# Inverse roots by ScalarE's square root and one Newton step in three places, by integer start and three Newton steps in the others; the opening's modulation dealt out by single weight blocks, with another order of transfers

## The chip, the cores and the metric

The kernel runs on one core of a Trainium2 chip. The metric is the device time of one execution in microseconds, of the slowest core; with one core it is that core's time. Five engines share the work and run their own queues in program order: TensorE (PE, matrix products, with PEld as its weight load), VectorE (DVE), ScalarE (ACT), GpSimd (POOL) and SyncE (SP), which here only issues transfers.

## The reference

One layer of a diffusion backbone over 512 latent tokens of width 1024 with a context of 256 tokens. It computes, cut to what matters here:

```
mod_x = split(silu(c) @ w_mod + b_mod, 6)          # six vectors of 1024; mod_c likewise from c_ctx
rms_norm(x, w) = x * rsqrt(mean(x*x) + 1e-6) * w
h   = rms_norm(x, mix_pre_norm) * (1 + mod_x[1]) + mod_x[0]
cq, ckv, kr, z, xbc, dt = split(h @ w_in)          # 384, 256, 32, 1024, 1536, 32
attn = latent attention (queries from rms_norm(cq), keys and values from rms_norm(ckv), context keys too)
ssd  = rms_norm(y * silu(z)),  y = two-way state-space scan over xbc, dt
x   = x + mod_x[2] * rms_norm([attn, ssd] @ w_out, mix_post_norm)
h   = rms_norm(x, ffn_pre_norm) * (1 + mod_x[4]) + mod_x[3]
gate, val = split(h @ w_up)                        # 2816 each
x   = x + mod_x[5] * rms_norm((gelu(conv3(gate)) * val) @ w_down, ffn_post_norm)
```

The context goes through the same first modulation and input projection (with mod_c), and gives keys, values and the scan's start states. Everything is fp32.

## The kernel before

**Products.** Each fp32 product is made of three faster ones. An operand is split into a high and a low part (`split`, L493 to L498: ACT copies the value to the rounded type, L497; DVE subtracts, L498), and TensorE adds high by high, high by low and low by high in one accumulator. The modulation and the token sums use plain fp32 products.

**Order.** The code is a recording: all instructions are first listed, then a planner (`price`, `dependences`, `Graph`, with lists of hints named `pins`, `urgent` and `holds`) prices each one, simulates the engines, chooses an order for every engine's queue, the transfers among them, and a place in memory for every block, and the program is built in that order. So an edit in one place lets the planner arrange all of it anew. `pins` fix one group of instructions behind another, `urgent` groups go first, and `holds` keep a group back. Loads are issued by SP (`load`, L489) except where `nc.scalar` is given, which is ACT's queue.

**Opening.** PE starts with dummy products on zeros (L677; `IDLE` gives their numbers in three places). Meanwhile the transfers bring c and c_ctx (as `cv`, and once more as `c2`), the transposed tokens `xt` in eight blocks of 128 columns by 512 tokens, the constants `cst` and the parameters `prm` (norm weights and b_mod). The steps:

- `spread` (L656) makes silu(c) a row over all partitions by eight products; the row stays in PSUM as `pv` and is copied to `cs`.
- `token_scale`: squares of the eight blocks on ACT (L608), their additions on DVE (L610), sums over the partitions by products with ones (L616), the mean (DVE, L620), the inverse root (`rsqrt`), eight products that lay the result out as rows over all partitions (`rows_of`, L534), and a copy of those rows, `rB`, by ACT (L627).
- The modulation is needed as a column per block k of 128 features: shift and scale. `modcolumn` loads a weight block (512 KB); `moddot` (L586) is a DVE product with the row of silu(c), summed along the row; `moddots` (L596) does it on PE instead, eight products of 128x64 per weight, for c and c_ctx at once. `ON_PE = 2, 4, 6` sends both weights of these blocks to PE; the other blocks' dots for c_ctx are done later, from the weights kept.
- `modulated` finishes a block: L632 adds b_mod, L633 multiplies (1 + scale) by the norm's weight, L638 scales the tokens by the column and by the row of inverse roots, L639 adds the shift and rounds to the high part (ACT), L642 makes the low part (DVE).
- `half_of_z` (L685): twelve products of the block with the first half of the z columns of w_in. The blocks come in the order `BLOCKS = 0, 2, 1, 4, 3, 6, 5, 7`. `silu_of_z` (L691, L692) and the second half of z follow.

**The inverse root.** All of them go through `rsqrt`, on a column (or four to six columns) of 128 values:

```
G.tensor_tensor(out=yt, in0=x, in1=powers[:, :n], op=ALU.pow)                      # L521, powers = -0.5
V.tensor_scalar(out=x, in0=x, scalar1=-0.5, scalar2=None, op0=ALU.mult)            # L522
V.scalar_tensor_tensor(out=tt, in0=yt, scalar=yt, in1=x, op0=ALU.mult, op1=ALU.mult)  # L524
V.scalar_tensor_tensor(out=yt, in0=tt, scalar=1.5, in1=yt, op0=ALU.add, op1=ALU.mult) # L528
```

that is, a power on POOL and one Newton step on DVE. It is used for the tokens and the context tokens (`token_scale`), for the two latents (cq and ckv), at the end of the scan (`ssd_finish`), twice for each of four token tiles around the output projection (`sumsq`), and once for each tile at the very end (`last`).

**Middle.** Input projections (`gemm_T`, L758), the scan, attention (L1181 to L1236), then the output projection (`natural_gemm`, L1295). The remaining modulation vectors are made by DVE dots beside it (`modblock`). `modfinish` turns the gate vector (with the norm's weight, L1275 to L1278) into a row: the column is written to DRAM in `mod_rows` (L1282) and read back to all partitions (L1284), both on ACT's queue:

```
nc.scalar.dma_start(out=scratch[n].rearrange("j p -> p j"), in_=ms)                # L1282
nc.scalar.dma_start(out=row, in_=scratch[n:n+1]... .to_broadcast([P, D]))          # L1284
```

**The turn into the MLP.** For each of four token tiles `after_mix` takes the sums of squares of the projection (ACT, L1347; L1349 or L1351), an inverse root, the product with the gate row (L1360; for the last tile's second half L1362 on ACT and L1363 on POOL), the residual (L1375), squares and an inverse root again, and the scaling by the row of 1 + scale (L1379). `transposes` (L1387) turns the tile, and L1390 and L1391 add the shift and make the high and low parts. Then come the up projection (`gemm_T`, L758, with `gated` behind it), and the down projection (L1482) with the last norm: squares L1502, the product with the gate row L1503, L1466, the inverse root, the residual L1472 and the store.

Of the kernel before, what the change touches and what calls it, by code (L numbers as in the profile page):

```python
# [18 lines left out]
P = 128  # L19
D = 1024  # L20
# [68 lines left out]
ON_PE = 2, 4, 6  # L89
BLOCKS = 0, 2, 1, 4, 3, 6, 5, 7  # L90
IDLE = 22, 26, 13
# [69 lines left out]
def price(x):  # L161
# [6 lines left out]
    if "DMA" in kind:  # L168
        words = any(len(v.bass_ap.ap) > 1 and v.bass_ap.ap[-1][0] != 1 for v in x.outs if hasattr(v, "bass_ap"))
        return DMA_WORDS if words else size(ops[0]) * ops[0][1][0][1] * 4 / 360  # L170
# [37 lines left out]
def table(x):  # L208

    return {AF.Tanh: 0, AF.Exp: 0, AF.Ln: 1, AF.Gelu: 2}.get(getattr(x, "func", None))  # L210
# [255 lines left out]
def build(nc, tc, ctx, a, out, dbg=None, places=None):  # L466
# [48 lines left out]
    powers = c_([P, 6], "powers")  # L515
    G.memset(powers, -0.5)

    def rsqrt(x, n):

        yt, tt = small(f"ry{n}", n), small(f"rt{n}", n)  # L520
        G.tensor_tensor(out=yt, in0=x, in1=powers[:, :n], op=ALU.pow)  # L521
        V.tensor_scalar(out=x, in0=x, scalar1=-0.5, scalar2=None, op0=ALU.mult)  # L522
        if n == 1:
            V.scalar_tensor_tensor(out=tt, in0=yt, scalar=yt, in1=x, op0=ALU.mult, op1=ALU.mult)  # L524
        else:
            V.tensor_tensor(out=tt, in0=yt, in1=yt, op=ALU.mult)
            V.tensor_tensor(out=tt, in0=tt, in1=x, op=ALU.mult)
# [12 lines left out]
    bk.cut(a=[two(0), two(2)], b=[bank(4), bank(5)], s=[bank(6)], m=[bank(7)])  # L540
    cv, cvp = t2(16, P), t2(P, P, dt=F32R)
    load(cv, a["cv"], nc.scalar)
    c2, cch, cc = c_([P, KD, 2], "c2"), c_([P, KD, 2], "cch"), c_([P, KD, 64], "cc")
# [9 lines left out]
    load(c2.rearrange("p a b -> p (a b)"), a["cc"])  # L553
# [22 lines left out]
    modc = c_([P, 16], "modc")  # L576
    sx, scx = c_([P, 16], "sx"), c_([P, 16], "scx")
# [10 lines left out]
    def moddots(k, w0, w1, pm):  # L588

        for n, w in enumerate((w0, w1)):  # L590
            began = here()
            at = BLOCKS.index(k) - 3 + n
            o = products[BLOCKS[max(at, 0)]] if at > -2 else rows
            pins.extend(((o[0] + i, o[0] + i + 2), (began, began + KD)) for i in range(0, o[1] - o[0], 2))
            for r in range(KD):
                mm(pm[:, 64 * n : 64 * n + 64], lhsT=w[:, r * P : (r + 1) * P], rhs=cc[:, r, :], start=r == 0,  # L596
                   stop=r == KD - 1)
        for n, md in enumerate((mod, modc)):
            V.tensor_tensor(out=md[:, k:16:8], in0=pm[:, n:128:64], in1=R("bmod", k, 9)[:, 0:9:8], op=ALU.add)
# [30 lines left out]
    def modulated(k, xt, rB, pr, md, aa, hi, lo):  # L630
# [9 lines left out]
        if not k:  # L640
            pfree(pr)
# [965 lines left out]
```

## Time and profile before

| what | us |
|---|---|
| times of three runs | 987.91, 988.67, 984.58 |
| their median | 987.91 |
| the profiled execution | 988.66 |
| its span in the trace | 986.9 |
| mean granted TensorE clock | 0.992 |

By stage, on the profiled execution (busy time of each engine in the stretch):

| stretch, us | what runs | PE | DVE | ACT | POOL | granted clock |
|---|---|---|---|---|---|---|
| 0 to 21 | opening | 17.34 | 11.12 | 9.61 | 2.16 | 0.84 |
| 21 to 58 | first half of z | 36.68 | 34.28 | 21.83 | 0.00 | 1.00 |
| 58 to 520 | rest of the input projection, scan, attention | 453.86 | 394.79 | 314.57 | 253.85 | 1.00 |
| 520 to 608 | output projection | 88.00 | 71.31 | 27.57 | 3.86 | 1.00 |
| 608 to 620 | turn into the MLP | 8.41 | 8.81 | 8.86 | 2.89 | 0.72 |
| 620 to 860 | up projection | 240.00 | 106.37 | 88.00 | 0.00 | 1.00 |
| 860 to 980 | down projection | 119.86 | 55.65 | 29.82 | 1.65 | 1.00 |
| 980 to 986.9 | last norm and store | 0.00 | 3.38 | 0.59 | 0.55 | 0.84 |

How to read it: times in the trace run from the span's start, in microseconds. A group's row gives line, engine, operation, written tile <- read tiles, shape, count, then busy time, the mean of one in ns, and the engine's idle time in front with what ended it. A row of the order in time gives start, duration, engine and line, and in brackets the idle time ahead of it and its releaser. A queue's row (SPq, ACTq) is the issue of a transfer. The granted clock is the share of full speed that TensorE was given.

### The profile page before, as it was taken

Reading aid. Unit: us, or ns where it says so; the run is one execution under the profiler, and the core shown is the slowest. Engines: PE = TensorE matmul, PEld = TensorE weight load, DVE = VectorE, ACT = ScalarE, POOL = GpSimd, SP = SyncE. Lnnn points to the kernel's source line nnn. Section 1 sums busy time; section 2 is a strip of 40 time slices with the busy share of each in tenths; the row PEclk is TensorE's granted clock in tenths of the full one; section 3 lists DMA queues with packets and bytes.
Section 4 is the critical chain, followed back from the end, with each engine's and each line's share of the span. In section 5 each row is a group of like instructions: output and inputs, shape, how many; then the busy total and the mean of one; then the engine's idle time right before and its main releaser. Section 6 shows DMA issues by size and latency. Waiting matters only on the chain. (4 is left out here: it accounts for less than half of the span.)

```text
span 986.9 us, 14324 instructions
## 1 busy us (share of the span) xinstructions
PE 964.1 (98%) x5213; PEld 824.1 (84%) x5213; DVE 685.7 (69%) x1181; ACT 500.8 (51%) x996; POOL 265.0 (27%) x238
## 2 busy tenths in 40 slices
PE   8999999999999999999999998999999999999997
PEld 8888888888878878889888887988888888888885
DVE  5999877896889999878789948925244342583504
ACT  4555347548569786878786114823232242652001
POOL 0002103756599986566440001000000000000000
PEclk8999999999999999999999999999999999999999
DMA  9923211012331341334577576332222312444422
GB/s 345 376 96 114 75 43 59 23 43 62 84 98 55 105 113 36 100 96 108 149 274 272 175 155 247 129 107 86 107 86 93 120 54 75 128 144 140 144 86 106
DMA packets 47542, 121.07 MB, mean 123 GB/s; under 512 B 9057, under 2 KB 12017, under 8 KB 47473
## 3 DMA queue, kind: packets, MB, share of 16 engines
q1 hardware_dynamic: 43744, 118.49, 37.4%
q10 hardware_dynamic: 3728, 1.68, 0.6%
q8 instruction: 41, 0.67, 0.3%
q14 instruction: 29, 0.23, 0.1%
HBM read 98.11 MB, written 6.30 MB: 106 GB/s over the span
## 5 line engine op out<-in xcount | busy, mean ns | idle before, releaser
L758 PE MATMUL banks<-block,block 128*128 128x512 f32 (+1 forms) x2132 | 449.7, 362 | 4.3 <-ACT block L1390 1.9
L758 PEld LDWEIGHTS banks<-block,block 128*128 128x128 f32 x2132 | 361.8, 190 | 65.6 <-ACT block L1390 2.1
L498 DVE TENSOR_TENSOR block<-block,block 128x512 fp32r<-128x512 f32 (+5 forms) x252 | 217.8, 890 | 105.3 <-ACT block L497 44.6
L497 ACT ACTIVATE block<-block 128x512 fp32r<-128x512 f32 (+4 forms) x252 | 180.7, 746 | 204.8 <-PE banks L1482 43.0
L521 POOL TENSOR_TENSOR smalls<-smalls,powers 128x1 f32<-128x1 f32 (+3 forms) x16 | 12.7, 792 | 507.0 <-DVE smalls L1466 359.3
L1482 PE MATMUL banks<-block,block 128*128 128x512 f32 x512 | 117.8, 389 | 0.0
L1482 PEld LDWEIGHTS banks<-block,block 128*128 128x128 f32 x512 | 96.1, 188 | 19.9
L1188 POOL TENSOR_TENSOR block<-block,smalls 128x768 f32<-128x768 f32 x64 | 95.4, 1498 | 51.9 <-DVE smalls L1187 32.7
L1181 PE MATMUL banks<-block,block 128*128 128x256 f32 (+1 forms) x384 | 95.3, 355 | 5.1 <-issue 1.9
L498 DVE TENSOR_TENSOR block<-banks,block 128x512 fp32r<-128x512 f32 (+1 forms) x156 | 83.2, 556 | 13.9 <-ACT block L497 12.5
L1295 PE MATMUL banks<-block,block 128*128 128x512 f32 x384 | 89.2, 390 | 0.0
L497 ACT ACTIVATE block<-banks 128x256 fp32r<-128x256 f32 (+1 forms) x156 | 74.0, 500 | 23.3 <-PE banks L1199 10.8
L1295 PEld LDWEIGHTS banks<-block,block 128*128 128x128 f32 x384 | 71.6, 188 | 14.7 <-DVE block L1236 0.2
L1181 PEld LDWEIGHTS banks<-block,block 128*128 128x128 f32 x384 | 59.7, 189 | 13.0 <-ACT block L1185 4.4
L1211 PE MATMUL banks<-block,block 128*128 128x256 f32 x384 | 68.7, 294 | 0.1
L1185 ACT ACTIVATE block<-banks,smalls 128x768 f32<-128x768 f32 x64 | 58.0, 907 | 14.4 <-DVE smalls L1183 10.1
L1183 DVE TENSOR_REDUCE smalls<-banks 128x1 f32<-128x768 f32 x64 | 60.8, 950 | 5.9 <-PE banks L1181 5.6
L586 DVE SCALAR_TENSOR_TENSOR block<-block,block 128x1024 f32<-128x1024 f32 x50 | 60.3, 1219 | 6.2 <-DMA block<-in_wmod_dram 6.1
L1199 PE MATMUL banks<-cst,block 128*128 128x128 f32 x384 | 63.2, 273 | 0.1
L1211 PEld LDWEIGHTS banks<-block,block 128*128 128x128 f32 x384 | 56.4, 189 | 4.6 <-ACT block L497 1.1
L793 DVE SCALAR_TENSOR_TENSOR block<-banks,cwh,block 128x510 f32<-128x510 f32 (+3 forms) x88 | 51.7, 621 | 11.3 <-ACT block L789 10.5
L1199 PEld LDWEIGHTS banks<-cst,block 128*128 128x128 f32 x384 | 46.5, 140 | 8.1 <-issue 2.2
(220 smaller groups left out, 1040.8 us busy)
## 6 DMA issues: line engine op xcount, KB each, us to landing
block<-in_wmod_dram SPq DMA_DIRECT2D x48, 512.0 KB, 6.2
block<-in_wup_dram SPq DMA_DIRECT2D x44, 512.0 KB, 4.5
block<-in_wdn_dram SPq DMA_DIRECT2D x44, 256.0 KB, 3.3
block<-block SPq DMA_DIRECT2D x32, 256.0 KB, 3.0
block<-in_wout_dram SPq DMA_DIRECT2D x16, 512.0 KB, 5.2
block<-block SPq DMA_DIRECT2D x56, 128.0 KB, 2.5
block<-in_wxbc_dram SPq DMA_DIRECT2D x12, 512.0 KB, 3.3
block<-in_wz_dram SPq DMA_DIRECT2D x16, 256.0 KB, 6.0
```

The source lines that it names most:

```text
L497: act(hi, src, AF.Copy)
L498: (lo_eng or V).tensor_tensor(out=lo, in0=src, in1=hi, op=ALU.subtract)
L586: V.scalar_tensor_tensor(out=junk, in0=wt, scalar=0.5, in1=vec, op0=ALU.mult, op1=ALU.mult, accum_out=acc)
L758: mm(po, lhsT=wf(k, pt[0]), rhs=xf(k, pt[1]), start=(k == 0 and pt == parts[0]), stop=(k == nk - 1 and pt == parts[-1]))
L1181: mm(sc[:, o : o + n], lhsT=q_[:, x_, qi * P : (qi + 1) * P], rhs=kk[:, y_, :], start=part == 0, stop=part == 2)
L1183: V.reduce_max(nm, sc[:, :T], axis=AX.X, negate=True)
L1185: act(pe, sc[:, :T], AF.Exp, bias=nm, scale=1.0, accum_out=sm_)
L1188: G.tensor_tensor(out=pe, in0=pe, in1=sm_.to_broadcast([P, T]), op=ALU.mult)
L1199: nc.tensor.transpose((tx if c < NX else tc_)[:, o : o + P], pe[:, s_ : s_ + P], ident)
L1211: mm(po[:, half * 256 : half * 256 + 256], lhsT=vst(c), rhs=rhs, start=(part == 0 and c == 0), stop=(part == 1 and c == NKT - 1))
L1295: mm(po[i][:, nh * 512 : nh * 512 + 512], lhsT=l[lp][:, i * P : (i + 1) * P], rhs=w[wp][:, nh * 512 : nh * 512 + 512], start=(k == 0 and l ...
L1482: mm(po[i], lhsT=l[lp][:, i * P : (i + 1) * P], rhs=w[wp], start=(k == 0 and lp == 0 and wp == 0), stop=(k == NF - 1 and lp == 1))
```

## The change

It does three things.

- **Inverse roots.** `rsqrt` loses its POOL power: it starts from an integer shift and subtraction on the number's bits and takes three Newton steps, all on DVE. It stays for the context tokens, the two latents and the scan's end. A new function `rsqrt_of` serves the tokens in the opening, `sumsq` at the turn and `last` at the end: ACT takes the square root of the scaled sum, DVE its reciprocal and one Newton step. The constants `powers` give way to `eps`. The planner's `table` learns of the square root, and a square root of no use (`small("root")`) stands ahead of the squares in the opening; ACT's table loads go from 6 to 10.
- **Modulation in the opening.** `ON_PE` names single weights, (block, 0 for shift or 1 for scale): five weights on PE instead of six, the blocks run in plain order, and every dot is followed by its own small addition (`modulation`, `dotted`), with b_mod + 1 for the scale made ahead (`bmod1`). The dots of block 1 are held until the first scaling. The copy `rB` is recorded behind block 0's scaling. `IDLE` goes from 22, 26, 13 to 22, 30, 20 dummies.
- **Transfers.** c2 (c and c_ctx as columns) moves from SP's queue, behind prm, to ACT's, behind cv; its tanh and the columns made of it are recorded ahead of `spread`. `xt` comes in three transfers of 512 KB and two of 256 KB. The planner's price of a transfer falls from bytes / 360 to bytes / 400.

```
-ON_PE = 2, 4, 6
-BLOCKS = 0, 2, 1, 4, 3, 6, 5, 7
-IDLE = 22, 26, 13
+ON_PE = (0, 1), (2, 0), (2, 1), (5, 0), (5, 1)
+IDLE = 22, 30, 20
...
-    return {AF.Tanh: 0, AF.Exp: 0, AF.Ln: 1, AF.Gelu: 2}.get(getattr(x, "func", None))
+    return {AF.Tanh: 0, AF.Exp: 0, AF.Ln: 1, AF.Gelu: 2, AF.Sqrt: 3}.get(getattr(x, "func", None))
...
     def rsqrt(x, n):
         yt, tt = small(f"ry{n}", n), small(f"rt{n}", n)
-        G.tensor_tensor(out=yt, in0=x, in1=powers[:, :n], op=ALU.pow)
+        V.tensor_scalar(out=yt.bitcast(I32), in0=x.bitcast(I32), scalar1=1, scalar2=None, op0=ALU.logical_shift_right)
         V.tensor_scalar(out=x, in0=x, scalar1=-0.5, scalar2=None, op0=ALU.mult)
+        V.tensor_scalar(out=yt.bitcast(I32), in0=yt.bitcast(I32), scalar1=-1, scalar2=0x5F3759DF, op0=ALU.mult, op1=ALU.add)
+        for _ in range(3):
+            if n == 1:
+                V.scalar_tensor_tensor(out=tt, in0=yt, scalar=yt, in1=x, op0=ALU.mult, op1=ALU.mult)
+            else:
+                V.tensor_tensor(out=tt, in0=yt, in1=yt, op=ALU.mult)
+                V.tensor_tensor(out=tt, in0=tt, in1=x, op=ALU.mult)
+            V.scalar_tensor_tensor(out=yt, in0=tt, scalar=1.5, in1=yt, op0=ALU.add, op1=ALU.mult)
+        return yt
...
+    def rsqrt_of(x, n, scale=1.0, more=None):
+        yt, tt, xh = small(f"ry{n}", n), small(f"rt{n}", n), small(f"rx{n}", n)
+        act(tt, x, AF.Sqrt, scale=scale, bias=eps[:, :1] if more is None else more)
+        if more is None:
+            V.tensor_scalar(out=xh, in0=x, scalar1=-0.5 * scale, scalar2=-0.5 * EPS, op0=ALU.mult, op1=ALU.add)
+        else:
+            V.tensor_scalar(out=xh, in0=x, scalar1=more, scalar2=-0.5, op0=ALU.add, op1=ALU.mult)
+        V.reciprocal(out=yt, in_=tt)
...
     load(cv, a["cv"], nc.scalar)
+    load(c2.rearrange("p a b -> p (a b)"), a["cc"], nc.scalar)
...
-    for k in range(KD):
-        load(xt[k // 2][:, k % 2, :], a["xt"][:, k, :])
+    for i in range(3):
+        load(xt[i], a["xt"][:, 2 * i : 2 * i + 2, :])
+    for i in range(2):
+        load(xt[3][:, i, :], a["xt"][:, 6 + i, :])
...
+    V.tensor_scalar(out=bmod1, in0=R("bmod", KD, KD), scalar1=1.0, scalar2=None, op0=ALU.add)
...
+    def modulation(k, n, raw, streams):
+        if n:
+            V.scalar_tensor_tensor(out=sx[:, streams, k], in0=raw, scalar=bmod1[:, k : k + 1],
+                                   in1=R("mixpre", k).to_broadcast([P, raw.shape[1]]), op0=ALU.add, op1=ALU.mult)
+        else:
+            V.tensor_scalar(out=shift[:, streams, k], in0=raw, scalar1=R("bmod", k), scalar2=None, op0=ALU.add)
+
+    def dotted(k, n, w, vec, stream):
+        raw = raws[:, 2 * stream + n, k : k + 1]
+        moddot(w, vec, raw)
+        modulation(k, n, raw, slice(stream, stream + 1))
...
             act(hi[:, h], xt[:, h], AF.Identity, bias=b_)
+            if not k and h.stop == rB.shape[1]:
+                act(rB, pr[:, : h.stop], AF.Copy)
...
+    act(cch, c2, AF.Tanh, scale=0.5)
+    V.scalar_tensor_tensor(out=c2, in0=cch, scalar=1.0, in1=c2, op0=ALU.add, op1=ALU.mult)
+    act(small("root"), cch[:, 0, :1], AF.Sqrt, scale=0.0, bias=eps[:, :1])
...
+        if k == 1:
+            holds.append((first, (later, here())))
...
-        return rsqrt(c0[0], 1)
+        V.tensor_scalar(out=c0[0], in0=c0[0], scalar1=D * EPS, scalar2=None, op0=ALU.add)
+        return rsqrt_of(c0[1], 1, 1.0, c0[0])
```

More of the change, by code (lines that the diff above doesn't have):

```diff
@@ L1458, in build, with last @@
     res = [t4() for _ in range(NX)]
[L1459 to L1461 removed]
+    sums = [small("dn", 2) for _ in range(NX)]
+    def last(i):
         ss = sums[i]
[L1464 to L1468 removed]
+        V.tensor_scalar(out=ss[:, 0:1], in0=ss[:, 0:1], scalar1=D * EPS, scalar2=None, op0=ALU.add)
+        c0 = rsqrt_of(ss[:, 1:2], 1, 1.0, ss[:, 0:1])
         xr = t4()
@@ L1505, in build @@
             if half:
-                last(i, 2)
+                last(i)
         pins.extend(zip(at, at[1:]))
```

117 lines of the change are left out of this document (53 added, 64 removed).

## The prediction, made before the changed kernel had run

> **What bounds the kernel now.** I read the busy shares first, then a table by stage, then the order in time where PE stops.
>
> ```profile
> PE 964.1 (98%) x5213; PEld 824.1 (84%) x5213; DVE 685.7 (69%) x1181; ACT 500.8 (51%) x996; POOL 265.0 (27%) x238
> ```
>
> PE is the bound; a shorter DVE, ACT or POOL pays only where PE waits. The table by stage (stretch in us; its length, then busy time of PE, weight load, DVE, ACT, POOL; granted clock; DMA share; GB/s) finds these places:
>
> ```profile
> 5.10:10.00 4.90, 4.87 (x39) 4.46 (x38) 3.57 (x7) 3.70 (x6) 0.30 (x1) 1.00 1.04 342
> 10.00:12.10 2.10, 0.01 (x2) 0.03 (x1) 1.97 (x5) 0.74 (x2) 0.00 (x0) 0.95 1.02 389
> 12.10:18.60 6.50, 6.50 (x30) 6.50 (x31) 3.83 (x16) 0.63 (x1) 1.03 (x1) 0.50 1.02 410
> 20.80:58.00 37.20, 36.84 (x202) 31.79 (x203) 34.46 (x71) 22.03 (x37) 0.00 (x0) 1.00 0.86 322
> 607.90:614.40 6.50, 2.94 (x20) 2.21 (x17) 4.05 (x12) 3.81 (x11) 1.57 (x3) 0.86 0.73 258
> 614.40:619.50 5.10, 5.07 (x24) 5.07 (x24) 4.63 (x14) 4.65 (x15) 0.90 (x2) 0.50 0.42 170
> 619.50:980.00 360.50, 360.36 (x1719) 303.21 (x1718) 162.25 (x244) 118.32 (x186) 2.07 (x4) 1.00 0.32 107
> 980.00:986.90 6.90, 0.00 (x0) 0.00 (x0) 3.38 (x8) 0.59 (x2) 0.55 (x1) 0.84 0.20 76
> ```
>
> There are three: the opening to 20.8, the turn into the MLP at 607.9 (after the output projection), and the 6.9 us behind the last product. The first two are followed by half clock (0.50). From 20.8 to 58 and from 619.5 to 980 PE is full, so work taken from PE there, or an earlier start, comes off the end one for one.
>
> **The opening.** In order of time (start, duration):
>
> ```profile
> 5.10 0.33 SPq L489 DMA_DIRECT2D prm<-in_prm_dram  x1
> 6.81 3.20 PE L677 MATMUL banks<-block 128*128 128x256 f32 x25
> 11.26 0.69 DVE L610 TENSOR_TENSOR block<-block,block 128x512 f32<-128x512 f32 x1
> 12.10 1.94 PE L616 MATMUL banks<-ones,block 128*128 128x64 f32 x8 [2.09 <-DVE block L610]
> 16.93 1.91 PE L534 MATMUL banks<-cst,smalls 128*128 128x128 f32 x8
> 18.63 1.94 PE L596 MATMUL banks<-cc,block 128*128 128x64 f32 x16
> 20.84 3.04 PE L685 MATMUL banks<-block,block 128*128 128x512 f32 x12 [0.26 <-ACT block L639]
> 58.24 1.05 PE L616 MATMUL banks<-ones,block 128*128 128x64 f32 x8
> ```
>
> The dummies of L677 end at 10.0, the token sums wait for the last addition of squares (11.95), and PE then runs at half clock to 18.6: the same eight records of L616 take 1.94 there and 1.05 at 58 us. The first input product stands at 20.84.
>
> Now the changed order, walked with these durations. The squares (L608) start later, behind a table load, but all eight still end by about 11:
>
> ```profile
> L608 ACT ACTIVATE block<-block 128x512 f32<-128x512 f32 x8 | 4.9, 627 | 1.3 <-DMA block<-in_xt_dram 1.0
> L649 ACT ACT_TABLE_LOAD x1 | 1.3, 1283 | 1.6 <-PEq L1572 1.6
> prm<-in_prm_dram SPq DMA_DIRECT2D x1, 126.5 KB, 5.2
> ```
>
> (the tanh of c, no longer behind prm, near 4.5; load 1.28; then eight squares, 4.9 in all.) What is late instead is DVE: the new addition on b_mod stands between the third and the fourth addition of squares and waits for prm, and the rest of the chain is queued behind it. prm lands at 5.10 + 5.2 = 10.3 now; the same 2.2 MB go ahead of it, in five transfers instead of eight. If the wide transfers run at the 410 GB/s of 12.1:18.6 rather than 342, it gains at most 0.5 us: 9.8. Behind it come four additions 0.6 apart (0.69 the last) and small ones: 9.8 + 2.75 = 12.55, the sums at 12.65 instead of 12.10. So the removal of the wait for cc does not show.
>
> From there PE's order decides: sums, seven eighths of weight (0,1), rows of the inverse root, the last eighth, 13 dummies, weight (2,0), first product. At half clock to 18.6: sums to 14.6; 14 records at 0.24 to 18.0; rows to 19.2 (three slow, the others at half that); 0.24; dummies 13 x 0.128 = 1.7; 1.92; first product at 23.1, which is 2.3 later. At full clock: 12.65 + 1.05 + 1.7 + 1.0 + 0.24 + 1.7 + 1.92 = 20.3, 0.5 earlier; the root itself (ACT's split of wz, square root, four small DVE operations, about 15.0) is ready by then, and weight (2,0) too: 2.9 MB behind prm at 410 GB/s is 7.1 us, 17.4.
>
> Behind the first product the change takes work from PE. Before, five of the six weights (eight products each, sixteen records) follow it; after, three of five, but seven dummies more:
>
> ```profile
> L596 PE MATMUL banks<-cc,block 128*128 128x64 f32 x96 | 11.5, 273 | 0.3 <-DVE modc L599 0.3
> L638 DVE SCALAR_TENSOR_TENSOR block<-block,sx,banks 128x256 f32<-128x256 f32 x2 | 0.9, 478 | 1.9 <-ACT block L627 1.9
> L642 DVE SCALAR_TENSOR_TENSOR block<-block,mod,block 128x512 fp32r<-128x512 f32 x8 | 6.0, 749 | 0.7 <-ACT block L639 0.7
> ```
>
> 11.5 / 6 = 1.92 a weight, twice: -3.8; dummies +0.9. The opening in sum: -0.6 at half clock, -3.4 at full clock. DVE keeps up: it has two dots (1.22) more behind the first scaling and one split (0.69) less, no longer waits 1.9 for the copy of L627, and starts 3.4 before the first product; PE needs the eighth block 28.7 after that product (84 products 21, weights 5.8, dummies 0.9, early second half 1.0), DVE takes some 31, so 1 us is spare. If that cover is gone, each us that DVE is late is PE's. I take half clock, **-0.6**: PE's gap shrinks only from 2.1 to about 1.7 us (30 dummies end near 10.9), the nearest row is the 10.0:12.1 one, and that was followed by 0.50.
>
> **The turn into the MLP.** The order in time; the view of mod_rows (its transfers' time to landing); two pieces of the chain of waits; two rows of the groups:
>
> ```profile
> 563.60 0.16 DVE L1278 TENSOR_TENSOR mod<-mod,prm 128x8 f32<-128x8 f32 x1
> 571.79 0.37 ACTq L1282 DMA_DIRECT2D mod_rows<-mod  x1
> 591.16 1.22 DVE L1360 TENSOR_TENSOR block<-banks,block 128x1024 f32<-128x1024 f32 x1 [8.24 <-DMA block<-mod_rows]
> 607.75 1.91 PE L1387 MATMUL banks<-cst,block 128*128 128x128 f32 x16
> 611.53 0.39 PE L758 MATMUL banks<-block,block 128*128 128x256 f32 x1 [1.87 <-ACT block L1390]
> 613.22 0.34 DVE L1391 SCALAR_TENSOR_TENSOR block<-banks,mod,block 128x128 fp32r<-128x128 f32 x1
> 614.43 5.35 PE L758 MATMUL banks<-block,block 128*128 128x256 f32 x24 [0.40 <-DVE block L1391]
> ...
> DMA to landing us min/median/max: 6.0/11.0/18.8
> ...
> 563.79 10.08 DMA mod_rows<-mod
> ...
> 573.89 17.18 DMA block<-mod_rows
> ...
> L586 DVE SCALAR_TENSOR_TENSOR block<-block,block 128x1024 f32<-128x1024 f32 x50 | 60.3, 1219 | 6.2 <-DMA block<-in_wmod_dram 6.1
> L498 DVE TENSOR_TENSOR block<-block,block 128x1024 fp32r<-128x1024 f32 x77 | 93.5, 1225 | 43.7 <-PE banks L758 23.3 <-ACT block L497 18.0 <-issue 1.8
> ```
>
> The last product of L1295 ends near 607.9. PE restarts in earnest at 614.43, for the low halves of L1391, which stand 22.1 us behind the arrival of the gate row at 591.1 in a DVE queue with little slack. The row's column was written from 563.79 in 10.1; its read at 573.89 took 17.2 and landed half a us behind the second column write (571.79 + 18.8 = 590.6) in the same queue. So the row's arrival sets the restart.
>
> The edit of the roots removes POOL's turn from each. In DVE's queue four small operations stay four, so the 22.1 become about 21.7 (each root saves some 0.5 in latency, most of it covered by other DVE work). More comes from the new order: between the last attention output and the first write stand 11 dots, 12 wide and 12 narrow splits instead of 12, 13 and 13 (about 1.2 + 1.15 + 0.6 = 3.0 us), and between the writes four dots instead of six (5.6 instead of 571.79 - 563.79 = 8.0). The second write goes out near 566.5, landing by 585.3 even at the slowest 18.8; the read, held by square, table load and root on ACT until about 574, lands at 580 (shortest, 6.0) to 586. Then 607.9 binds instead: the first low half near 607.9 + 2.2 (tile 3's multiplication 0.7, tile 2's scaling 1.3), the second by 611.6. Restart 611.6 instead of 614.4: **-2.8**; the bounds are -0.3 (row at 591 as now) and, downward, the rival below. The half clock behind the gap I leave, since a gap of 3.7 us remains.
>
> **Tail and the other roots.**
>
> ```profile
> 980.75 0.68 DVE L1503 TENSOR_TENSOR block<-banks,block 128x512 f32<-128x512 f32 x1
> 980.91 0.55 POOL L521 TENSOR_TENSOR smalls<-smalls,powers 128x1 f32<-128x1 f32 x1 [4.68 <-DVE smalls L1466]
> 981.50 0.15 DVE L522 TENSOR_SCALAR smalls<-smalls 128x1 f32<-128x1 f32 x1
> L1187 DVE RECIPROCAL smalls<-smalls 128x1 f32<-128x1 f32 x64 | 9.2, 155 | 8.9 <-ACT block L1185 8.3
> ```
>
> POOL's 0.55 already lies under L1503; after, reciprocal (0.155) and two more stand behind the same L1503. **-0.1**. The roots left to DVE (context, both latents, four of the scan's end) become nine or twelve small operations of about 0.16 instead of three or four and a POOL turn: 1.0 to 1.3 us more DVE each. No PE wait hangs on them now (DVE is 69% busy); between nothing and 1 us for each of the two latents I take **+0.4**. Two of the four added table loads lie in ACT's idle time in front of the turn and the tail, one in the scan's stage under products. In a sentence apart: the Trainium skill (ScalarE: Activation LUTs, What ACT_TABLE_LOAD costs) adds a drain of 1.38 us to the 1.28 of each load; the squares would end near 11.8, the last addition near 12.7, and the sum would be worse by about 0.15.
>
> Sum: -0.6 - 2.8 - 0.1 + 0.4 = -3.1. The profiled run took 988.66 (span 986.9), 0.75 over the median 987.91; taken off the median: **984.8**.
>
> **Rivals.** 1. *The opening stays at full clock.* For it: 30 dummies instead of 25, the gap under 2 us. Against: 2.1 us were enough to halve it. Opening -3.4: 982.0. The Trainium skill (TensorE: Matmul & The Clock Gate, What's actually happening) would have it so: half clock only after an idle window of about 3.4 us; the 0.50 at 12.1 after 2.1 us idle speaks against this. 2. *The turn doesn't move.* The row lands at 591 as now, since the read also waits behind a square and a table load: -0.6 - 0.3 - 0.1 + 0.4, 987.3. 3. *The row comes later, slower than before.* Both writes now leave together into one queue ahead of the read. If each takes the 18.8 measured under traffic, one behind the other from 560.8, the row lands at 598.9, the low halves 21.7 later, the restart near 622: +7.5 instead of -2.8, 995.1. It decides from a row later than about 591.5. For it: the second write took 18.8. Against: the first took 10.1 with the same loads waiting beside it.
>
> **Numbers.** Forecast 0.38, rival 1 0.24, rival 2 0.15, rival 3 0.16; the rest, 0.07, is a PE wait elsewhere, since everything is planned anew, mostly on the slow side. The range 980.0 to 992.0 takes in rivals 1 and 2, 2 us on the fast side for both clocks staying full, and on the slow side the first half of rival 3, up to a row some 6 us later than now; the forecast's own range is 983 to 987. About 0.5% (4.9 us) is what a measurement can tell from no change, so faster means under 983.0: rival 1 and a third of the forecast, 0.37. Slower, over 992.8, takes most of rival 3 and part of the rest: 0.18. Same 0.45.
>
> **What would show it.** Right: three weights behind the first product and that product at 20 to 23; prm's landing ahead of the b_mod addition; the second column write near 566.5 and the gate row ahead of 586; PE's stop at the turn near 3.7 us. Wrong: a first product past 24, DVE late for the eighth block, a gate row past 591.5, or new PE waits between 60 and 520.

## The result, and the profile after

The changed kernel is slower: 994.5 us (median of 5 runs, 993.89 to 995.59) against 985.57 us of the kernel before beside it. The ratio is 1.0083, 95% interval 1.0063 to 1.0104. The profiled execution spans 993.8 us, 6.9 more than before's 986.9. (In both kernels the profiled execution was the slowest run.)

The busy shares first, of the changed kernel, then PE's order in time at the opening and at the turn (start, duration, in brackets idle time and its releaser):

```profile
PE 964.4 (97%) x5208; PEld 824.2 (83%) x5208; DVE 704.3 (71%) x1235; ACT 509.0 (51%) x1014; POOL 253.3 (25%) x219
```

```profile
8.39 1.55 PE L691 MATMUL banks<-block,sel 128*128 128x128 f32 x8 [2.39 <-DVE sel L593]
9.73 4.91 PE L713 MATMUL banks<-block 128*128 128x256 f32 x30
15.02 1.08 PE L651 MATMUL banks<-ones,block 128*128 128x64 f32 x8 [0.37 <-DVE block L645]
21.93 3.24 PE L721 MATMUL banks<-block,block 128*128 128x512 f32 x13
...
58.16 1.10 PE L651 MATMUL banks<-ones,block 128*128 128x64 f32 x8
...
609.74 2.82 PE L1429 MATMUL banks<-cst,block 128*128 128x128 f32 x12 [2.40 <-DVE block L1421]
618.00 1.01 PE L801 MATMUL banks<-block,block 128*128 128x256 f32 x3 [5.43 <-ACT block L1432]
620.60 5.91 PE L801 MATMUL banks<-block,block 128*128 128x256 f32 x26 [1.59 <-DVE block L1433]
```

PE does the same work (964.4 against 964.1 us busy); it waits more. Read against the lines of before:

| place (profiled executions, us) | before | after |
|---|---|---|
| first input product | 20.84 | 21.93 |
| sums of the context's squares | 58.24 | 58.16 |
| last product of the output projection ends | 607.92 | 606.91 |
| PE restarts in earnest | 614.43 | 620.60 |
| last product of the down projection ends | 979.86 | 987.07 |
| span | 986.9 | 993.8 |

Up to the end of the output projection nothing is lost (1.0 is gained). All of the loss, 8.2 us, lies between that and the end of the down projection: 380.16 instead of 371.94. The tail gives 0.3 back.

What PE waited for at the turn is in the two other queues. The order in time of ACT (with its transfer issues) and DVE, of the changed kernel:

```profile
559.82 6.16 ACTq L1325 DMA_DIRECT2D mod_rows<-mod  x2
569.11 1.03 ACT L1390 ACTIVATE block<-banks 128x1024 f32<-128x1024 f32 x1 [9.94 <-DVE block L611]
570.24 1.28 ACT L538 ACT_TABLE_LOAD   x1
570.26 1.82 ACTq L1327 DMA_DIRECT2D block<-mod_rows  x1
571.53 0.29 ACT L538 ACTIVATE smalls<-smalls,eps 128x1 f32<-128x1 f32 x1
592.69 0.34 ACTq L1327 DMA_DIRECT2D block<-mod_rows  x1
609.77 1.03 ACT L1390 ACTIVATE block<-banks 128x1024 f32<-128x1024 f32 x1 [2.12 <-DVE block L1421]
```

```profile
565.41 0.17 DVE L1321 TENSOR_TENSOR mod<-mod,prm 128x8 f32<-128x8 f32 x1
594.88 1.22 DVE L1402 TENSOR_TENSOR block<-banks,block 128x1024 f32<-128x1024 f32 x1 [16.06 <-DMA block<-mod_rows]
618.20 0.34 DVE L1433 SCALAR_TENSOR_TENSOR block<-banks,mod,block 128x128 fp32r<-128x128 f32 x1
620.20 0.34 DVE L1433 SCALAR_TENSOR_TENSOR block<-banks,mod,block 128x128 fp32r<-128x128 f32 x1
```

The view of mod_rows and the chain of waits give the transfers:

```profile
DMA to landing us min/median/max: 4.5/10.2/27.0
```

```profile
570.26 24.52 DMA block<-mod_rows
```

The first column write goes out at 559.82, the second is ready at 565.41 + 0.17, and both stand ahead of the read of the gate row. So they did in before (writes at 563.79 and 571.79, read at 573.89); what is new is that the second one goes out 6 us earlier. The first takes 10.4 (the read of it is issued at 570.26). The second takes 27.0: the read that waits for it is issued at 592.69. The gate row lands at 594.8, 24.5 after its issue and some 2 us behind the second write. DVE has stood idle for 16.06 by then; the first low half comes 23.3 later (618.20), the second at 620.20, with an inverse root of the last tile and a residual between them, and PE restarts. From 618.0 to 627.4 it ran at a granted clock near half (0.50 and 0.56 in the table by stage), as before's did from 614.4 to 619.5.

These rows split the loss of 8.2 us. PE's stop, from the end of the output projection to the restart, grew from 6.5 to 13.7 us: 1.0 because the projection ended earlier and the row did not, 3.7 because the row came later (594.88 against 591.16), and 2.5 because the way from the row to the restart is longer, 25.7 instead of 23.3. (The first low half stands 23.3 behind the row instead of 22.1, the restart 2.4 behind the first low half instead of 1.2.) The last 1.0 lies behind the restart, where a clock near half lasts 6.8 us instead of 5.1.

### The profile page after: what moved, and what is told of

Same layout as the page of the kernel before. It is cut to its first block, busy times and chain, and to the rows that moved or that the text cites. A ratio compares the mean times of both kernels' runs of the same rounds, so it can differ in the third digit from the quotient of the medians.

```text
span 993.8 us, 14359 instructions
## 1 busy us (share of the span) xinstructions
PE 964.4 (97%) x5208; PEld 824.2 (83%) x5208; DVE 704.3 (71%) x1235; ACT 509.0 (51%) x1014; POOL 253.3 (25%) x219
## 5 line engine op out<-in xcount | busy, mean ns | idle before, releaser
L801 PE MATMUL banks<-block,block 128*128 128x512 f32 (+1 forms) x2132 | 447.7, 362 | 7.0 <-ACT block L1432 5.4
L497 DVE TENSOR_TENSOR block<-block,block 128x512 fp32r<-128x512 f32 (+4 forms) x252 | 227.5, 932 | 76.1 <-PE banks L801 39.6
L496 ACT ACTIVATE block<-block 128x512 fp32r<-128x512 f32 (+5 forms) x252 | 180.3, 742 | 182.6 <-PE banks L801 38.4
L1224 PE MATMUL banks<-block,block 128*128 128x512 f32 (+1 forms) x384 | 96.5, 354 | 2.8 <-ACT block L1228 1.8
L497 DVE TENSOR_TENSOR block<-banks,block 128x256 fp32r<-128x256 f32 (+1 forms) x156 | 83.1, 554 | 6.0 <-ACT block L496 3.6
L611 DVE SCALAR_TENSOR_TENSOR block<-block,block 128x1024 f32<-128x1024 f32 x53 | 63.5, 1218 | 10.9 <-DMA block<-in_wmod_dram 10.9
L1242 PE MATMUL banks<-cst,block 128*128 128x128 f32 x384 | 65.8, 275 | 0.2 <-DVE block L497 0.2
L1464 DVE SCALAR_TENSOR_TENSOR block<-banks,prm,block 128x511 f32<-128x511 f32 x22 | 16.4, 749 | 60.3 <-ACT block L1463 60.3
```

The source lines that it names most:

```text
L496: act(hi, src, AF.Copy)
L497: (lo_eng or V).tensor_tensor(out=lo, in0=src, in1=hi, op=ALU.subtract)
L611: V.scalar_tensor_tensor(out=junk, in0=wt, scalar=0.5, in1=vec, op0=ALU.mult, op1=ALU.mult, accum_out=acc)
L801: mm(po, lhsT=wf(k, pt[0]), rhs=xf(k, pt[1]), start=(k == 0 and pt == parts[0]), stop=(k == nk - 1 and pt == parts[-1]))
L1224: mm(sc[:, o : o + n], lhsT=q_[:, x_, qi * P : (qi + 1) * P], rhs=kk[:, y_, :], start=part == 0, stop=part == 2)
L1242: nc.tensor.transpose((tx if c < NX else tc_)[:, o : o + P], pe[:, s_ : s_ + P], ident)
```

## The experiments

Every run was timed against the kernel before on the same chip. A run "planned anew" lets the planner arrange the whole program; one "in its own plan" keeps the order of every queue but for the entry named. For all of them one measure is shown beside the ratio: the time from the last product of the output projection to the last of the down projection ("MLP with turn"). The products in it are the same in all kernels, so it tells what the turn cost, with the clock that follows it.

| run | ratio to before, 95% | end of output projection, us | MLP with turn, us |
|---|---|---|---|
| before | 1 | 607.9 | 371.9 |
| after | 1.0083 [1.0063, 1.0104] | 606.9 | 380.2 |
| after_write_late | 1.0074 [1.0050, 1.0097] | 609.9 | 379.0 |
| before_write_late | 1.0004 [0.9990, 1.0018] | 606.8 | 374.5 |
| after_pow | 1.0044 [1.0028, 1.0061] | 608.8 | 375.1 |
| before_sqrt | 0.9942 [0.9925, 0.9960] | 604.4 | 369.4 |
| after_price20 | 1.0103 [1.0077, 1.0129] | 616.6 | 373.0 |
| before_price20 | 1.0075 [1.0053, 1.0097] | 614.9 | 373.2 |
| before_sqrt_price20 | 1.0063 [1.0044, 1.0081] | 617.7 | 370.9 |
| after_rate360 | 0.9996 [0.9982, 1.0009] | 605.7 | 374.1 |
| after_rows_given | 0.9971 [0.9958, 0.9985] | 609.4 | 368.2 |
| before_rows_given | 0.9939 [0.9915, 0.9964] | 609.2 | 367.9 |
| before_rate400 | 1.0040 [1.0024, 1.0056] | 606.0 | 378.1 |
| after_rate440 | 1.0070 [1.0044, 1.0096] | 608.1 | 379.7 |
| after_turned | 0.9913 [0.9891, 0.9934] | 605.7 | 367.2 |
| before_turned | 0.9924 [0.9903, 0.9944] | 602.0 | 368.7 |
| before_sqrt_turned | 0.9951 [0.9935, 0.9967] | 610.5 | 367.4 |
| before_sqrt_rows_given | 0.9910 [0.9890, 0.9931] | 605.7 | 367.9 |

**1. The second write behind the read**, in the plan of each kernel:

```diff
-ACT's queue: ..., write 0, write 1, square, root, read 0, ..., read 1
+ACT's queue: ..., write 0, square, root, read 0, write 1, ..., read 1
```

> The changed kernel with one entry of ACT's queue moved: the second column write to mod_rows (L1325) goes out behind the read of the gate row (L1327) instead of ahead of it. Theory: the gate row lands late because its read stands in one transfer queue behind that write, which took 27.0 us here (565.6 to 592.6). Then the row lands by 584 instead of 594.8, the output projection's end at 607.3 binds, PE restarts at 612 to 614 instead of 620.6, and the time falls by 6 to 8 us, from 994.5 to 987 to 988.5. Rival: the loads of SP piled up behind the first write (seven of 512 KB) hold the row back, whatever the queue's order: the row still lands past 590 and the time stays within 2 us of 994.5.

> The kernel before with the same move: second column write (L1282) behind the read of the gate row (L1284). Theory: the row lands by 585 instead of 591.1, PE restarts near 611.6 instead of 614.4, about 2.8 us off: 982 to 983. Rival (pile of loads): row at 590 or later, no change.

Neither time moved. The chain of waits of after_write_late shows why:

```profile
562.78 10.59 DMA mod_rows<-mod
573.39 0.35 ACTq L1327
...
573.76 25.06 DMA mod_rows<-mod
598.84 4.79 DMA block<-mod_rows
...
603.73 1.30 DVE block L1421
```

The first row did come early: DVE used it at 583.21 in after_write_late and at 582.93 in before_write_late, 11.7 and 8.2 us sooner. But the second write, behind the read now, took 25.1 (17.2 in before_write_late), and the second row, the scale, came at 603.6 (598.9). It is needed at L1421, one step after the first. But it is not the row that DVE waited for longest. The order in time of ACT and DVE in after_write_late:

```profile
598.84 0.33 ACTq L1327 DMA_DIRECT2D block<-mod_rows  x1
599.29 1.06 ACT L496 ACTIVATE block<-block 128x1024 fp32r<-128x1024 f32 x1 [14.35 <-DMA block<-in_wup_dram]
```

```profile
601.42 0.21 DVE L542 TENSOR_SCALAR smalls<-smalls,eps 128x1 f32<-128x1 f32 x1 [14.53 <-ACT block L1390]
603.73 1.28 DVE L1421 SCALAR_TENSOR_TENSOR block<-block,smalls,block 128x1024 f32<-128x1024 f32 x1 [0.23 <-DMA block<-mod_rows]
```

The read of the second row stands in ACT's own queue. It went out at 598.84, when the second write had landed, and a split and the square of the first tile, which came behind it in that queue, started at 599.29 and 600.26. DVE waited 14.53 for that square and then 0.23 for the row; in before_write_late 7.04 and 2.43. (The trace puts these 14.35 of ACT down to a load of weights; where the queue goes the same way, it names the write: 13.63 in the changed kernel, 7.00 in before, 7.40 in before_write_late.) So the theory was right on the first row and wrong on what follows: the wait went to what stands behind the second write, ACT's next operations and the second row. The rival, the loads alone, fell too: the first row came well before 590.

**2. Which part of the change.** The roots undone in the changed kernel (after_pow), and done alone in the kernel before (before_sqrt), both planned anew:

```diff
-act(tt, x, AF.Sqrt, ...); V.reciprocal(out=yt, in_=tt); one Newton step
+G.tensor_tensor(out=yt, in0=x, in1=powers[:, :n], op=ALU.pow); one Newton step
```

> The changed kernel with the inverse roots of before (power on POOL, one Newton step on DVE) in all places, planned anew; the opening's changes stay. If the roots cost the 9 us, it goes to 985 to 987 and the gate row lands near 591 as before; if the new plan's place of the column writes does it, whatever the root, the second write still leaves ahead of the first read and well before 571.8, the row lands near 594, and the time stays at 992 to 995. PE's first input product stays near 22, since it waits for the squares, not for the root.

> The kernel before with the changed roots (ScalarE's square root for tokens, turn and end; integer start and three steps elsewhere), planned anew; the opening stays as before. If the roots cost the 9 us, 992 to 995. If not, within 2 us of 985.6, with the time set by where the plan puts the second column write: behind 571, as before, no change; ahead of 567, a row past 592 and 3 us or more lost.

Opposite signs: the roots cost 0.4% on the changed opening (1.0083 against 1.0044) and gain 0.6% on the old one. Beside the sizes of the roots (two or three operations of 0.15 to 0.3 us in each) that is too much either way. In the first pair the last column carries all of it (380.2 against 375.1); in the second it carries less than half (369.4 against 371.9), and the rest is an output projection that ends 3.5 us earlier. after_pow took the time expected if the place of the writes does it, but not by that mechanism: its second write went out at 571.6, as late as before's, and the row was used at 590.3, not near 594. In before_sqrt the plan had put the first write 4 us earlier (559.3) and the second behind the read (570.60 against 570.16), so that the first tile's product with the row ran at 581.43, before the second write had landed (586.5).

**3. The price of a transfer.** The changed kernel with the old price, the kernel before with the new one, and the changed kernel with a third:

```diff
-        return DMA_WORDS if words else size(ops[0]) * ops[0][1][0][1] * 4 / 400
+        return DMA_WORDS if words else size(ops[0]) * ops[0][1][0][1] * 4 / 360
```

> The changed kernel with the old price of a transfer (bytes / 360), planned anew. If the new price set the bad turn, the second write leaves behind the first read again, and the time comes back to 985 to 988 (ratio 0.998 to 1.002). If not, 993 to 996 (1.006 to 1.010).

> The kernel before with nothing changed but the planner's price of a transfer (bytes / 400 instead of / 360), planned anew. If the price by itself does the harm, as its undoing in the changed kernel suggests, ratio 1.004 to 1.010, with both column writes ahead of the first read and the first row past 592. If it does harm only together with the changed opening, 0.998 to 1.002.

> The changed kernel with bytes / 440, which makes another plan of the same work; here too both writes are queued ahead of the first read. If that order is what loses the time, 1.005 to 1.010 as with / 400. If each plan is a draw of its own, it may land anywhere from 0.994 to 1.010, and the place of the writes doesn't foretell it.

One number in the planner, which changes no operation, takes the whole loss out of the changed kernel (0.9996) and puts 0.4% into the kernel before. In the changed kernel two things make this up: in after_rate360 the output projection ends 2.2 us earlier than in before, and its turn is still 2.2 us worse. There the second write went out at 576.7, behind the first read (566.5); in after_rate440 and before_rate400 both writes stood ahead of it, as in the changed kernel. The order alone doesn't decide, though: in before, too, both stand ahead of it. The chain of waits in before_rate400:

```profile
569.79 19.53 DMA mod_rows<-mod
589.39 6.07 DMA block<-mod_rows
```

and in after_rate440:

```profile
582.83 15.21 DMA block<-mod_rows
```

The first row came at 595.5 and 598.0, and the MLP with its turn took 378.1 and 379.7.

**4. Without the slow writes and the late rows.** The two rows are read from an input matrix, so that their reads wait for no write, and the column writes go out in 32 bytes a partition; each kernel keeps its own plan. This takes out three things at once: the lateness of the rows, ACT's waiting ahead of a read, and what the slow writes do to other transfers. The rows hold other values than the gate and the scale.

```diff
-nc.scalar.dma_start(out=scratch[n].rearrange("j p -> p j"), in_=ms)
-nc.scalar.dma_start(out=row, in_=scratch[n : n + 1]....to_broadcast([P, D]))
+nc.scalar.dma_start(out=scratch[n].rearrange("j (q i) -> (j q) i", i=8), in_=ms)
+nc.scalar.dma_start(out=row, in_=a["wout"][0][n : n + 1, :].to_broadcast([P, D]))
```

> The changed kernel in its own plan, every queue in the same order, but the two rows of the turn are read from an input matrix instead of from mod_rows, and their column writes go out as 32 bytes a partition instead of 4 bytes a value; the rows so hold other values than the gate and the scale. This leaves out only the lateness of the rows. Theory: the late row is the 9 us; without it the first row is there by 580, the end of the output projection near 607 binds, PE restarts by 613 and the time falls to 985 to 988 (ratio to before 0.998 to 1.002). Rival: the order of DVE and ACT behind the row (a root between squares) costs as much by itself: restart past 616, ratio 1.004 or more.

> The same in the kernel before: rows from an input matrix, short column writes, own plan. Theory: its row at 591 sets the restart at 614.4 too, so 2 to 4 us are to be had: ratio 0.996 to 0.998. If DVE's own chain sets it, no change.

> The opening of before with the changed roots in its own plan, rows read from an input matrix and short column writes as in before_rows_given. If the roots gain by themselves, 0.986 to 0.990; if only by the place of the rows, 0.992 to 0.995, as in before_rows_given (0.994).

PE at the turn in after_rows_given, in the order in time:

```profile
609.20 1.91 PE L1431 MATMUL banks<-cst,block 128*128 128x128 f32 x16
611.33 0.62 PE L801 MATMUL banks<-block,block 128*128 128x256 f32 x3 [0.22 <-ACT block L1434]
613.25 3.72 PE L801 MATMUL banks<-block,block 128*128 128x256 f32 x26 [1.31 <-DVE block L1435]
```

The same queues in the same order, and the stops of 2.40, 5.43 and 1.59 us are none, 0.22 and 1.31; the 26 products behind them take 3.72 instead of 5.91, at full clock (1.00 from 609.4 to 618). The changed kernel falls from 1.0083 to 0.9971, the kernel before to 0.9939, before_sqrt from 0.9942 to 0.9910; the MLP with its turn takes 368 in all three. So the slow writes, with the late rows, cost the changed kernel 1.1% (about 11 us), the kernel before 0.6% (6 us) and before_sqrt 0.3%. They are the turn's loss: without them the changed kernel's last column falls by 12.0 and that of before by 4.1, a difference of 7.9 out of 8.2. The rival, that the order of DVE and ACT behind the row costs as much by itself, falls. Of the 0.83% between the two kernels 0.3% is left without the slow writes (0.9971 against 0.9939), with intervals that just overlap (0.9958 to 0.9985 and 0.9915 to 0.9964). The first two came out below the ranges expected of a late row, before_sqrt_rows_given between its two.

**5. A truer price for the column writes**, planned anew:

```diff
-DMA_START, DMA_WAIT, DMA_AHEAD, DMA_ALONE, DMA_WORDS = 650, 910, 3000, 0.8, 5000
+DMA_START, DMA_WAIT, DMA_AHEAD, DMA_ALONE, DMA_WORDS = 650, 910, 3000, 0.8, 20000
```

> The changed kernel, but the planner counts 20 us for a column write to mod_rows instead of 5 (the traces show 10.1 to 27.0), planned anew. Theory, revised after the first four runs: moving one write only moves the wait from the first row to the second; what costs is that the turn's queues are ordered for rows that come 10 to 20 us earlier than they do. Then both writes go out by 550 instead of 559.8 and 565.6, both rows are there by 580, the output projection's end near 607 binds, PE restarts by 612 instead of 620.6, and 994.5 falls by 7 to 10 us (ratio to before 0.992 to 1.000). Rival: the rows don't bind, the ScalarE root's place in ACT's queue between the squares does: restart at 618 or later, time within 2 us of 994.5.

> The kernel before with the same price. Theory: rows by 580, restart by 612 instead of 614.4, 2 to 4 us faster than before (ratio 0.996 to 0.998). Rival: no change, 0.999 to 1.001.

> The opening of before, the changed roots, and the price of 20 us. Theory: the turn's order is already good in the run without the price (restart 607.6, second row at 595), so 0 to 3 us more: ratio to before 0.990 to 0.995. If the good turn there was the luck of one plan, another plan may lose it: 0.998 or more.

All three missed what the theory gave, on the slow side; only the last had a branch for it (0.998 or more). The writes did go out at 540 to 546 and 557 to 560, and the first row was there by 580; but the projection itself ended at 615 to 618 instead of 607. In after_price20 PE was busy 448.87 of the 462 us from 58 to 520, against 454.02 in the changed kernel, with two waits, of 2.01 at 487 (on a split) and of 4.13 at 497 (on a transfer between two blocks):

```profile
497.62 1.62 PE L1224 MATMUL banks<-block,block 128*128 128x512 f32 x3 [4.13 <-DMA block<-block]
```

The other two runs have their longest wait of the attention on the same kind of transfer, 2.47 and 2.44 near 500 and 505. Work for the rows had been pulled forward into the attention: from 440 to 520 after_price20 issued 14 loads of 512 KB of modulation weights instead of 9 (before_price20 15 instead of 11), and from 440 to 560 it made 16 dots instead of 12. That these loads are what held up the transfers is likely from this, but no run shows it by itself. In these three plans making the rows early by working earlier cost more than their lateness. And the turn still took 371 to 373 us, though no engine waited for a row, against 368 in experiment 4; what else costs there the runs don't show.

**6. Cheaper column writes.** The column (128x8) is put into a 128x32 tile, turned by VectorE in 32x32 blocks, and written in pieces of 128 bytes; planned anew.

```diff
-            V.tensor_tensor(out=ms, in0=ms, in1=R(nrm, 0, 8), op=ALU.mult)
+            V.tensor_tensor(out=turn[n % 2][0][:, :8], in0=ms, in1=R(nrm, 0, 8), op=ALU.mult)
+        V.transpose(out=turn[n % 2][1], in_=turn[n % 2][0])
-            nc.scalar.dma_start(out=scratch[n].rearrange("j p -> p j"), in_=ms)
+            nc.scalar.dma_start(out=scratch[n].rearrange("j (g i) -> g j i", i=32), in_=turn[n % 2][1])
```

> The changed kernel with the modulation columns turned by one VectorE transposition of 32 by 32 blocks each and written to mod_rows as 128 pieces of 128 bytes instead of 1024 of 4, planned anew. If the 4-byte writes are the cause, a write takes some 3 us instead of 10 to 27, both rows are there by 580, and the 9 us are gone: ratio to before 0.994 to 1.000. If not, 1.004 or more.

> The kernel before with the same turned columns, planned anew. If the cause holds, as with given rows: 0.992 to 0.997. If not, 0.999 or more.

> The opening of before, the changed roots, turned columns. If the roots gain by themselves, 0.986 to 0.991, below before_turned; if they gained only by the place of the rows, the same as before_turned, 0.992 to 0.997.

The same output is computed, and all three beat both kernels: 0.9913 (below the range expected), 0.9924 and 0.9951; about 980 us for the first two. ACT's queue in before_turned:

```profile
559.13 1.10 ACTq L1286 DMA_DIRECT2D mod_rows<-tr  x1
562.18 1.03 ACT L1351 ACTIVATE block<-banks 128x1024 f32<-128x1024 f32 x1 [6.74 <-DMA mod_rows<-tr]
562.20 0.37 ACTq L1288 DMA_DIRECT2D block<-mod_rows  x1
565.82 0.53 ACTq L1286 DMA_DIRECT2D mod_rows<-tr  x1
569.19 0.33 ACTq L1288 DMA_DIRECT2D block<-mod_rows  x1
```

A write takes 3.1 and 3.4 us (559.13 to the read at 562.20, 565.82 to 569.19) where the 4-byte form took 10 to 27; in after_turned the second one, with loads beside it (253 and 345 GB/s in the two stretches from 570 to 580), took at most 7.7 (573.12 to the read at 580.81). The changed kernel and the kernel before are now equal (the intervals lie over each other). before_sqrt_turned misses what was expected if the roots gain by themselves: its turn is as good as the others', but its output projection ends at 610.5.

## Why the prediction was wrong, point by point

The forecast was 984.8, -3.1 off the median; measured were 994.5 and +0.8%. It was the third rival that came, a row later than before behind two writes: row at 594.8 (598.9 was worked out), restart at 620.6 (622), time 994.5 (995.1). It had been given 0.16. That its numbers come so near is partly luck: it took 18.8 for each write, where the first took 10.4 and the second 27.0, and the row, 4.1 earlier than it had worked out, was followed by a way to the restart of 25.7 us instead of some 23.

- **The turn (-2.8 forecast, +8.2 measured): this is the step that failed.** "The second write goes out near 566.5" was right (565.6). That it would be "landing by 585.3 even at the slowest 18.8" was not: it took 27.0, and the read, queued behind it, landed with it. The 18.8 was taken for an upper bound because it was the largest in one view of one execution. The way behind the row was mis-sized as well: the first low half was to come 21.7 behind it, and came 23.3 behind it. The argument against the rival, that the first write took 10.1 "with the same loads waiting beside it", misread the row: those loads were waiting, not running. Two stretches of the table by stage (last three columns granted clock, DMA share, GB/s) show it, of the changed kernel:

```profile
564.00:570.00 6.00, 6.00 (x28) 4.97 (x27) 5.90 (x12) 0.89 (x1) 0.00 (x0) 1.00 0.52 20
575.00:580.00 5.00, 5.00 (x24) 4.13 (x23) 2.63 (x5) 1.06 (x1) 0.00 (x0) 1.00 1.18 304
580.00:584.00 4.00, 4.00 (x19) 3.34 (x18) 0.00 (x0) 0.00 (x0) 0.00 (x0) 1.00 0.99 93
```

  and of after_turned, whose writes go out at 567.08 and 573.12:

```profile
564.00:570.00 6.00, 6.00 (x28) 4.95 (x28) 5.97 (x16) 0.00 (x0) 0.00 (x0) 1.00 0.52 175
575.00:580.00 5.00, 5.00 (x24) 4.14 (x23) 1.93 (x5) 1.34 (x2) 0.00 (x0) 1.00 0.95 345
```

  While the first column is written, the DMA engines are half busy and move 20 GB/s: 4-byte pieces, with nearly no load beside them. Then the loads that have piled up run (304), and the second column lands behind them, at 592.6. So we read the first write's 10 us as the time of a write that has the engines, and the second's 27 as that of one behind a pile. The other runs of the 4-byte form fit: in seven of them, where the first write went out 5.8 us or more ahead of the second, its read could follow 10.1 to 11.0 behind it; in before_rate400, where the second went out 1.5 behind the first and the transfers moved 66 to 204 GB/s from 570 to 590, the first took 19.5, and in after_rate440, with 204 GB/s from 565 to 570, its read went out 17.3 behind it. The second writes took 12 to 27.
- **What moved the second write forward** was put down to fewer dots and splits ahead of it. The runs show that the planner's price of a transfer is enough to move it, which the prediction didn't weigh as a term: with the old price the write goes out at 576.7, behind the read, and the loss is gone (0.9996), though roots, opening and transfers are the changed ones. That the plan is sensitive is not the mechanism, though; the mechanism is the 4-byte write (experiments 4 and 6).
- **The opening (-0.6 forecast, -0.1 in the profiled pair).** The size is near, the steps were not. "All eight squares end by about 11" and "the sums at 12.65" came out as 12.5 and 15.02. ACT's order in time of the changed kernel:

```profile
6.51 0.22 ACT L695 ACTIVATE cch<-c 128x16 f32<-128x16 f32 x1 [1.26 <-DMA c<-in_cc_dram]
6.74 1.28 ACT L697 ACT_TABLE_LOAD   x1
8.04 0.29 ACT L697 ACTIVATE smalls<-cch,eps 128x1 f32<-128x1 f32 x1
8.24 4.25 ACT L643 ACTIVATE block<-block 128x512 f32<-128x512 f32 x8
```

  The tanh of c was set near 4.5; its transfer landed at 6.5, and the table load and all squares stand behind it. The constants, third on ACT's queue, came late as well, so PE waited 2.39 for the cast of sel (8.39). PE did run at full clock from the sums on, so rival 1 was right on the clock there and no gain came of it. The half clock had only moved ahead of the sums, onto the dummies behind that wait of 2.39 (0.50 in the table by stage), whose 30 took 4.91 us and ended at 14.64, where 10.9 was forecast:

```profile
10.00:12.00 2.00, 2.00 (x11) 2.00 (x11) 1.77 (x5) 2.00 (x5) 0.00 (x0) 0.50 1.02 400
```

  Over all profiles the sums at 58 us stand at 57.2 in the mean of the six kernels with before's opening and roots and at 58.9 in the eight with the changed opening: it costs some 1.7 us rather than gaining 0.6.
- **The table load.** The row of L538 above (570.24, 1.28 long, the root at 571.53) and that of L697 (6.74, the next at 8.04, begun as L695 ends at 6.73) show no further drain of 1.38 us, which the Trainium skill (ScalarE: Activation LUTs, What ACT_TABLE_LOAD costs) adds; the trace does not agree.
- **Tail (-0.1 forecast):** 7.04 before (979.86 to 986.9), 6.73 after: -0.3.
- **Integer roots (+0.4 forecast):** nothing shows. DVE's busy time from 58 to 520 us rose by 18 us, the PE's stays, as the row of the changed kernel says beside before's 453.86 and 394.79:

```profile
58.00:520.00 462.00, 454.02 (x2755) 393.12 (x2755) 412.98 (x740) 316.53 (x696) 250.56 (x208) 1.00 0.31 90
```

- **Open:** whether the new roots gain anything of their own. They came out at 0.3% better with rows given (0.9910 against 0.9939, intervals that overlap) and 0.3% worse with turned columns (0.9951 against 0.9924, likewise). And why the output projection ends anywhere from 602 to 610 in plans that differ little: small PE waits of 6 to 10 us in all between 58 and 520, in other places in each, were seen but not traced to a cause.

## What to carry to other kernels

A transfer's time to landing, read from one execution, is the time of that neighbourhood. Before it is used as a bound for a moved transfer, look at what ran beside it: GB/s and DMA share over the same stretch. A DRAM write of a column in 4-byte pieces is a thing to remove (turn it on chip first), not to schedule around: moving it moved the wait, starting it earlier cost more. And where a planner orders the whole program, compare a change with a run that changes only a price in the planner; here that alone was worth +0.4% to +0.9%, as much as the change of the roots (-0.6% and +0.4%). And a read that waits for a write holds up all that its issuing engine has behind it: put it where nothing urgent follows. No run here tried that.

## What the runs showed of the hardware

- A column of 1024 values written to DRAM in 4-byte pieces took 10 to 27 us, and while the first one ran all transfers together moved 13 to 25 GB/s, though loads had been issued (25 from 564 to 570 and 13 from 570 to 575 in before); in 128-byte pieces, with four times the bytes, 3 to 4 us in before_turned and up to 7.7 in after_turned, where 345 GB/s were moved beside the second one (575 to 580).
- A transfer that waits for another holds up its engine's queue: in the changed kernel ACT started nothing from 579.5 until the read of the second row had gone out at 592.69, and the trace puts the 13.63 us down to the write.
- Whether a gap of PE is followed by half clock does not hang on its length alone. The same gap ahead of the token sums, 2.09 us in before, was followed by a granted clock of 0.50 to 18.6; in before_turned it is 2.33 us, and the clock stays whole (table by stage):

```profile
12.00:14.00 2.00, 1.75 (x15) 1.77 (x16) 1.40 (x8) 0.20 (x1) 0.32 (x1) 1.00 1.04 413
16.00:18.00 2.00, 2.00 (x21) 2.00 (x20) 1.58 (x6) 1.39 (x2) 0.00 (x0) 1.00 1.03 410
```

  The first input product then stands at 18.57 instead of 20.84. So some 2 us of the scatter between executions lie in the opening, without a change of its order: before_write_late, with before's order there, had it at 18.82.
